# x comes transposed as well, the first column group multiplies it before the norm, and u is normalised in place

## The chip, the cores and the metric

The kernel runs on one core of a Trainium2 chip. The metric is the device time of one execution in microseconds, as the median of several runs. Four engines are named below: TensorE (PE in the profile; PEld is its weight loads), VectorE (DVE), ScalarE (ACT) and GpSimd (POOL). SyncE (SP) issues the transfers, one after the other.

## The reference

One layer takes 512 tokens and 16 meta tokens of width 1024 in fp32, normalises them, projects them to eleven column groups, runs a retention branch and a gated linear attention (GLA) branch on them, merges the two, adds the residual and normalises again. What bears on the change is its start:

```python
u = rms_norm(h, norm_gain)          # u = h * r * gain, r = 1/sqrt(mean(h*h) + eps) per token
proj = u @ w_in
(rq, rk, rv, rg, gq, gk, gv, gg, glr, m_ret, m_gla) = jnp.split(proj, points, axis=-1)
...
gq = gq.reshape(bsz, length, GLA_HEADS, GLA_K_DIM) * (GLA_K_DIM ** -0.5)
gk = gk.reshape(bsz, length, GLA_HEADS, GLA_K_DIM)
gv = gv.reshape(bsz, length, GLA_HEADS, GLA_V_DIM)
log_a = jax.nn.log_sigmoid((glr @ w_gate_up + b_gate)) / GLA_GATE_TAU
```

Since r is one number per token, (h * gain) @ w scaled row by row with r is the same product as u @ w.

## The kernel before

**Products.** Every fp32 product is made from three products of reduced precision. `split` (L139 to 141) casts a tile to a high part on ACT (L140) and subtracts it from the tile on another engine, DVE unless told otherwise, for the low part (L141). `mm3` (L152, L155, L156) multiplies high by high, low by high and high by low. Six buffers hold raw weights, three hold high and low parts. PSUM has two pools of four banks, `pp` and `pa`.

**Tokens.** The 528 tokens are held as two halves of 264 (256 tokens and 8 meta tokens). The activations lie transposed, as 128 features by 264 tokens, four such blocks side by side. `fh` and `fl` hold their high and low parts in seven forms: A11, A12, A22 and (as `a21h`, `a21l`) A21 are the blocks of u, S1 to S4 are sums and differences of them, which `quad` uses to make a 2 by 2 block product with seven products instead of eight.

**The start, in program order.** x is loaded in four blocks of 128 rows and one of 16 meta rows (L409 to 419), each followed on SP by a piece of the first weight, `gv0`. Then for every block (L435 to 455): squares and their sum on ACT (L436), r by `rstd_of` on DVE and POOL (L163, L164), the multiply `xn` = x * r * gain on DVE with the gain broadcast to all partitions (L439), eight transposes of 128x128 on TensorE (L444), and from their PSUM banks the split into fh and fl and a copy into `u` (L452, L453). Then the four sums (L472 to 475) and their splits.

**After that.** `forget_gates` loads its small weight (`fg_f`, L492), multiplies u by it (`glr`, 32 products), then makes the gate logits `z` (five products) and from them `la` through exponentials and logarithms on ACT and DVE. `gla_v(0)` makes the first 512 columns of gv with `proj_b` (96 products of 128x512, in four pieces `gv_0` to `gv_3` of the weight) and the meta rows (`gv_pm`, 8 products). `gla_qk(0)` makes gq and gk with `proj_a` (96 products each). Then `gla_g(0)`, a `quad` (products gg_1, gg_2, gg_6, gg_7, gg_5 and so on, 24 each), runs together with `gla_attention(0)`: `ge`, `gf` (sums of la, from its high and low parts `lah`, `lal`), `gm` (the same for the meta rows), `gc` (scores from gQ and gK). The other column groups, the retention branch, the merge and the output projection follow.

**What sets the order.** `weave` takes turns between a generator of products and one of a chain of small steps: one step of the chain for each step of the products, from the third argument on. Within that, the tile framework places instructions on each engine's queue; an engine works its queue in order. `pin` holds the products of one group behind those of the one before. A tile taken from a pool whose memory another tile still uses waits for that tile's last reader: the pool `gp` lies over the memory of `xp`, which holds x, xn, the sums and the other tiles of the start.

Of the kernel before, what the change touches and what calls it, by code (L numbers as in the profile page):

```python
# [106 lines left out]
def hybrid_kernel(ctx: ExitStack, tc: tile.TileContext, I, out: bass.AP):  # L107
# [23 lines left out]
    ggain = cp.tile([P, 16], F32, name="ggain")  # L131
# [43 lines left out]
    def run(*gens):  # L175
        for g in gens:
            yield from g
# [139 lines left out]
    def proj_b(src, col, left, name, evac, meta=None):  # L317

        pss = [ppt(f"{name}_p{t}") for t in range(NTB)]
        psm = pat(f"{name}_pm") if meta is not None else None  # L320
        raws = []
        for q in range(4):
# [4 lines left out]
            if name == "gv0":  # L327
                for kk in range(2):
                    split(hi[:, kk, :], lo[:, kk, :], raw[:, kk, :], nc.gpsimd)
            else:  # L330
                split(hi, lo, raw)
            raws.append(raw)
            for t in range(NTB):
                for kk in range(2):
                    k = 2 * q + kk
                    mm3(pss[t], *left(k, t), hi[:, kk, :], lo[:, kk, :], k == 0, k == KD - 1, True)
                if q == 3:
                    evac(t, pss[t])
                if t == 1:
                    run_late()  # L340
                    yield
            if psm is not None and q % 2 == 1:
                for g in range(4):
                    k = 2 * (q - 1) + g
                    nc.tensor.matmul(psm[32 * g:32 * g + 32], um[:, k, :], raws[q - 1 + g // 2][:, g % 2, :],
                                     start=q == 1, stop=q == 3)
            if q == 3 and psm is not None:
                late.append(lambda: meta(psm))
            yield

# [52 lines left out]
    gmask = g1.tile([P, 3, P], I32, name="gmask")  # L403

# [4 lines left out]
    blocks = [(I["x"][t * P:(t + 1) * P, :], P, t * P) for t in range(NTB)]  # L409
    blocks.append((I["meta_tokens"], NM, T))  # L410
    xts = []
    ngb = xp.tile([P, D], F32, name="ngb", bufs=1)
    for n, (src, rows, t0) in enumerate(blocks):
        xts.append(xp.tile([P, D], F32, tag="xt", name=f"xt{n}", bufs=5))
        nc.sync.dma_start(xts[n][:rows], src)
        if n == 0:
            nc.sync.dma_start(ngb, I["norm_gain"].to_broadcast([P, D]))
        if n < NTB:
            load_b(w_in, C_GV, n, "gv0")
# [3 lines left out]
    wps = pat("warm_p")  # L423

    def warm(n):
        for _ in range(n):
            nc.tensor.matmul(wps, wzero[:, :P], wzero, start=True, stop=True)

    warm(14)
    nc.gpsimd.memset(um, 0.0)  # L430
    u = xp.tile([P, 2, 2, 4, HT], F32, name="u", bufs=1)
    for n, (src, rows, t0) in enumerate(blocks):
        xt = xts[n]
        sq = xp.tile([P, D], F32, tag="sq", name=f"sq{n}")
        ss = sp.tile([P, 1], F32, tag="ss", name=f"ss{n}")  # L435
        nc.scalar.activation(sq[:rows], xt[:rows], AF.Square, accum_out=ss[:rows])  # L436
        r = rstd_of(ss[:rows], D, rows, f"n{n}")
        xn = xp.tile([P, D], F32, tag="xn", name=f"xn{n}")
        nc.vector.scalar_tensor_tensor(xn[:rows], xt[:rows], r[:rows], ngb[:rows], op0=ALU.mult, op1=ALU.mult)  # L439
        for g in range(2):  # L440
            pt = pat(f"xt{n}_{g}")
            for e in range(4):
                k = 4 * g + e
                nc.tensor.transpose(pt[:, e * P:e * P + rows], xn[:rows, k * P:(k + 1) * P], ident[:rows, :rows])  # L444
            v = pt.rearrange("p (e t) -> p e t", e=4)[:, :, :rows]
            if rows == NM:
# [7 lines left out]
        if n == 0:  # L454
            warm(3)
# [621 lines left out]
```

## Time and profile before

| what | us |
|---|---|
| median of 3 runs | 822.55 (821.91 to 823.01) |
| the profiled execution, its own time | 823.74 |
| its span in the trace | 822.0 |
| TensorE busy in the span | 790.3 |
| first gv0 product | 10.89 |
| gate logits z | 55.10 |
| first gg product | 86.02 |
| second gg_b group (gg_5) | 102.52 |

The span is what the trace covers; the execution's own time is 1.7 longer. A row of a timeline gives start, duration, engine, source line, operation, output tile<-operand tiles, shape and count, and in brackets the idle time of the engine ahead of it with what ended it. A wait of several things is put down to the last of them.

### The profile page before, as it was taken

What the parts mean: (1) busy time and instruction counts of PE and PEld (TensorE: products, weight loads), DVE (VectorE), ACT (ScalarE), POOL (GpSimd) and SP (SyncE); (2) the same over time, 40 slices, a digit from 0 to 9 for tenths busy, and PEclk for the clock granted to TensorE, in tenths of its full rate; (3) what the DMA queues carried; (4) which work ended last, traced back from release to release, by engine and by line L of the source; (5) the groups of instructions that cost most, each with busy time, mean ns of one, the idle gap of its engine ahead of it and who ended that gap; (6) DMA issues with size and microseconds to landing.
All of it is one profiled execution on the core that took longest, in us unless ns stands there. A gap on an engine that the chain in (4) does not pass through costs nothing.

```text
span 822.0 us, 13635 instructions
## 1 busy us (share of the span) xinstructions
PE 790.3 (96%) x5466; PEld 719.3 (88%) x5466; DVE 541.5 (66%) x775; ACT 407.7 (50%) x673; POOL 147.3 (18%) x186
## 2 busy tenths in 40 slices
PE   6898999999999999999999999999999998999896
PEld 3687988998887999998999989999899998998685
DVE  3758666577643398766677576766757778885922
ACT  6564585357744336525445354453444555553422
POOL 4500243005331240013000141002410010021031
PEclk9998999999999999999999999999999999999999
DMA  9240330033335803521426237261472267589402
GB/s 282 82 115 26 90 90 3 26 103 103 111 120 143 193 26 103 176 82 65 143 76 185 72 72 151 66 198 57 85 146 71 84 218 230 179 184 249 146 0 103
DMA packets 84679, 95.62 MB, mean 116 GB/s; under 512 B 7988, under 2 KB 71732, under 8 KB 84616
## 3 DMA queue, kind: packets, MB, share of 16 engines
q1 hardware_dynamic: 78984, 86.36, 34.4%
q0 software_dynamic: 5632, 8.39, 7.0%
q8 instruction: 43, 0.70, 0.4%
q14 instruction: 20, 0.16, 0.1%
HBM read 77.96 MB, written 16.78 MB: 115 GB/s over the span
## 4 chain that ended last, share of the span: by engine, by line
PE 75%; DVE 6%; DMA 4%; ACT 4%; issue 2%; POOL 2%; SPq 0%; POOLq 0%; DVEq 0%; ACTq 0%
PE rk_p L297 6%; PE rg_b L225 6%; PE rq_p L297 6%; PE rv_b L225 5%; PE gk_p L297 3%; PE rg_c L225 3%; PE br_p L155 3%; PE br_p L152 3%; PE br_p L156 3%; PE rv_c L225 2%; PE mg_b L225 2%; DMA mk<-kept 2%; PE gg_b L225 2%; PE wo_p L152 2%; PE wo_p L156 2%
## 5 line engine op out<-in xcount | busy, mean ns | idle before, releaser
L164 POOL TENSOR_TENSOR g_r<-g_v,mhalf 128x1 f32<-128x1 f32 x16 | 10.3, 646 | 265.4 <-DVE g_v L163 265.4
L152 PE MATMUL br_p<-oh,br_h 128*128 128x512 f32 x128 | 50.1, 391 | 0.5 <-DVE mt L974 0.5
L155 PE MATMUL br_p<-ol,br_h 128*128 128x512 f32 x128 | 50.3, 393 | 0.0
L156 PE MATMUL br_p<-oh,br_l 128*128 128x512 f32 x128 | 50.1, 391 | 0.0
L141 DVE TENSOR_TENSOR rg_l<-rg_w,rg_h 128x1024 fp32r<-128x1024 f32 x24 | 30.0, 1252 | 17.9 <-ACT rg_h L140 17.9
L141 DVE TENSOR_TENSOR rv_l<-rv_w,rv_h 128x1024 fp32r<-128x1024 f32 x24 | 29.4, 1224 | 15.8 <-ACT rv_h L140 15.8
L914 ACT ACTIVATE on<-av,nm,g_r 128x512 f32<-128x512 f32 x16 | 12.5, 778 | 52.6 <-DVE nm L912 52.6
L140 ACT CAST rv_h<-rv_w 128x1024 fp32r<-128x1024 f32 x24 | 25.3, 1052 | 23.9 <-issue 7.3
L225 PE MATMUL rv_b<-rv_h,fh 128*128 128x256 f32 x128 | 36.3, 284 | 0.0
L225 PE MATMUL rg_b<-rg_l,fh 128*128 128x256 f32 x128 | 36.0, 281 | 0.0
L225 PE MATMUL rv_b<-rv_h,fl 128*128 128x256 f32 x128 | 36.0, 281 | 0.0
L225 PE MATMUL rv_b<-rv_l,fh 128*128 128x256 f32 x128 | 36.0, 281 | 0.0
L140 ACT CAST rg_h<-rg_w 128x1024 fp32r<-128x1024 f32 x24 | 25.2, 1052 | 21.6 <-PE br_p L155 11.6
L225 PE MATMUL rg_b<-rg_h,fl 128*128 128x256 f32 x128 | 35.9, 281 | 0.0
L225 PE MATMUL rg_b<-rg_h,fh 128*128 128x256 f32 x128 | 35.8, 280 | 0.0
L639 POOL COPY gto<-gX 128x1 f32<-128x1 f32 x16 | 8.5, 530 | 122.9 <-ACT gX L629 122.9
L152 PEld LDWEIGHTS br_p<-oh,br_h 128*128 128x128 f32 x128 | 24.0, 188 | 6.1 <-issue 0.9
L638 POOL TENSOR_TENSOR gQ<-gX,gq 128x512 f32<-128x512 f32 x16 | 28.3, 1768 | 3.9 <-ACT gX L631 3.9
L152 PE MATMUL wo_p<-wo_h,mh 128*128 128x512 f32 (+1 forms) x72 | 26.9, 374 | 2.0 <-DVE mt L974 2.0
L156 PEld LDWEIGHTS br_p<-oh,br_l 128*128 128x128 f32 x128 | 24.0, 188 | 5.2
L155 PEld LDWEIGHTS br_p<-ol,br_h 128*128 128x128 f32 x128 | 24.0, 188 | 5.0
L297 PE MATMUL rk_p<-fh,rk_h 128*128 128x264 f32 x96 | 27.6, 287 | 0.0
(490 smaller groups left out, 3098.2 us busy)
## 6 DMA issues: line engine op xcount, KB each, us to landing
rg_w<-in_w_in_dram SPq DMA_DIRECT2D x16, 512.0 KB, 4.2
rv_w<-in_w_in_dram SPq DMA_DIRECT2D x16, 512.0 KB, 3.9
br_w<-in_w_branch_ret_dram SPq DMA_DIRECT2D x16, 512.0 KB, 4.1
gv_w<-in_w_in_dram SPq DMA_DIRECT2D x8, 512.0 KB, 3.6
gg_w<-in_w_in_dram SPq DMA_DIRECT2D x8, 512.0 KB, 4.5
bg_w<-in_w_branch_gla_dram SPq DMA_DIRECT2D x8, 512.0 KB, 3.5
rq_w<-in_w_in_dram SPq DMA_DIRECT2D x8, 512.0 KB, 4.2
rk_w<-in_w_in_dram SPq DMA_DIRECT2D x8, 512.0 KB, 4.6
```

Of the source, the lines that this page charges most:

```text
L140: nc.scalar.copy(hi, src)
L141: eng.tensor_sub(lo, src, hi.bitcast(F32))
L152: m = nc.tensor.matmul(o, lh, rh, start=first, stop=False)
L155: nc.tensor.matmul(o, lh, rl, start=False, stop=False)
L156: m = nc.tensor.matmul(o, ll, rh, start=False, stop=last)
L164: nc.gpsimd.tensor_tensor(r[:rows], v[:rows], mhalf[:rows], op=ALU.pow)
L225: m = nc.tensor.matmul(ps[:, t, :], l, r, start=first and j == 0, stop=kk == 3 and j == 2, skip_group_check=not fresh or t == 1)
L297: m = nc.tensor.matmul(pss[t][th], l[:, kk, c], r, start=first and j == 0, stop=kh == 1 and kk == 3 and j == 2, skip_group_check=not meta ...
L638: nc.gpsimd.tensor_mul(Q[b, h], X[:, 0:4, :], qb)
L639: nc.gpsimd.tensor_copy(TO[b, h], X[:, 0, P - 1:P])
L914: nc.scalar.activation(on, ps, AF.Identity, scale=r, bias=nm)
```

## The change

The host hands over x a second time, transposed and in the two halves with their meta tokens (`xt`, 128 x 8 x 2 x 264), and the three gains laid out by column. The transposed x goes straight into `u`. From it come `xgh` and `xgl`, the high and low parts of x * gain, made by eight instructions on ACT and eight on DVE. gv0 multiplies these, without the norm, and its evacuation on ACT scales each token's row by r.

The norm runs beside that in a new generator, `activations`. x in rows is still loaded for its squares. r stands on the diagonal of a tile `dg`; a matrix of ones times `dg` leaves r in all partitions of a PSUM bank `rb`; 16 instructions on DVE multiply u by gain and `rb` in place. fh and fl of u are then split from u in blocks of 128x1056, and the sums are made in the buffer of `xgh`. The 32 transposes, the copies into u, the broadcast load of the gain (512 KB) and the tiles `xn` go. The low parts of gv0's weights are subtracted on DVE instead of POOL. The meta rows of gv0 follow its last product in one run of eight. The first twelve products on zeros, which run before data is there, replace 14 + 3. `gla_v(0)` is woven with `activations`, and `forget_gates` with `gla_qk(0)` alone. `gv` and `gvm` move to a pool of their own memory, since `gp` is opened later.

```diff
     def proj_b(src, col, left, name, evac, meta=None):
...
             if name == "gv0":
                 for kk in range(2):
-                    split(hi[:, kk, :], lo[:, kk, :], raw[:, kk, :], nc.gpsimd)
+                    split(hi[:, kk, :], lo[:, kk, :], raw[:, kk, :])
...
-            for t in range(NTB):
-                for kk in range(2):
-                    k = 2 * q + kk
-                    mm3(pss[t], *left(k, t), hi[:, kk, :], lo[:, kk, :], k == 0, k == KD - 1, True)
-                if q == 3:
+            steps = [(t, kk) for t in range(NTB) for kk in range(2)]
+            if q == 0:
+                steps.sort(key=lambda x: x[1])
+            for n, (t, kk) in enumerate(steps):
+                k = 2 * q + kk
+                mm3(pss[t], *left(k, t), hi[:, kk, :], lo[:, kk, :], k == 0, k == KD - 1, True)
+                if q == 3 and kk == 1:
                     evac(t, pss[t])
...
+        if meta is not None:
+            psm = pat(f"{name}_pm")
+            for k in range(KD):
+                g = k % 4
+                nc.tensor.matmul(psm[32 * g:32 * g + 32], um[:, k, :], raws[k // 2][:, k % 2, :],
+                                 start=k < 4, stop=k >= 4)
...
+    nc.sync.dma_start(ng, I["norm_gain"])
+    for q in range(4):
+        nc.sync.dma_start(u[:, 2 * q:2 * q + 2], I["xt"][:, 2 * q:2 * q + 2])
+        load_b(w_in, C_GV, q, "gv0")
+        for n in ((), (0, 1), (2, 3), ())[q]:
+            nc.sync.dma_start(xr[n], I["x"][n * P:(n + 1) * P, :])
+        if q == 1:
+            nc.sync.dma_start(xr[4][:NM], I["meta_tokens"])
...
+    for k in range(KD):
+        g = ng[:, k:k + 1]
+        nc.scalar.activation(xgh[:, k], u[:, k], AF.Copy, scale=g)
+        nc.vector.scalar_tensor_tensor(xgl[:, k], u[:, k], g, xgh[:, k].bitcast(F32),
+                                       op0=ALU.mult, op1=ALU.subtract)
...
+    def norm(n, rows=P):
         ss = sp.tile([P, 1], F32, tag="ss", name=f"ss{n}")
+        nc.scalar.activation(xr[n][:rows], xr[n][:rows], AF.Square, accum_out=ss[:rows])
+        norms[n] = rstd_of(ss[:rows], D, rows, f"n{n}")
+        dg = xp.tile([P, P], F32, tag="dg", name=f"dg{n}", bufs=3)
+        nc.vector.tensor_scalar_mul(dg[:rows, :rows], ident[:rows, :rows], norms[n][:rows])
+        return dg
+
+    def activations():
+        dgm = norm(4, NM)
+        for th in range(2):
+            rb = pat(f"rb{th}")
+            for i in range(2):
+                nc.tensor.matmul(rb[:, i * P:(i + 1) * P], ones, norm(2 * th + i), start=i == 0, stop=True,
+                                 skip_group_check=i > 0)
...
+            for g in range(2):
+                for k in range(4 * g, 4 * g + 4):
+                    nc.vector.scalar_tensor_tensor(u[:, k, th, :], u[:, k, th, :], ng[:, k:k + 1], rb[:, :HT],
+                                                   op0=ALU.mult, op1=ALU.mult)
+                split(ah[th, g][:, :, :HT], al[th, g][:, :, :HT], u[:, 4 * g:4 * g + 4, th, :])
+            nc.vector.tensor_copy(um[:, :, th * HM:(th + 1) * HM], u[:, :, th, 256:HT])
+            yield
...
+        sums = xp.tile([P, KD, 2, HT], F32, tag="xgh", name="sums", bufs=1).rearrange("p (i k) h t -> p i (k h) t", i=4)
...
+            split(fh[i][:, :, :HT], fl[i][:, :, :HT], ss[i])
+            yield
...
         if p == 0:
-            yield from proj_b(w_in, C_GV, left, "gv0", lambda t, ps: nc.scalar.copy(v[:, t, :], ps), meta)
+            yield from proj_b(w_in, C_GV, left, "gv0", lambda t, ps: nc.scalar.activation(
+                v[:, t, :], ps, AF.Copy, scale=norms[t]), meta)
...
+    weave(gla_v(0), activations(), 3)
+    xctx.close()
+    gp = gctx.enter_context(tc.tile_pool(name="gp", bufs=1, reuse_waits="tile"))
...
-    weave(run(gla_v(0), gla_qk(0)), forget_gates(), 4)
+    weave(gla_qk(0), forget_gates(), 1)
```

Three places show how instructions move. The first is the split of gv0's last weight piece, `gv_3_l`. Before, it stood on POOL; its neighbours there are small casts of constants and the meta rows' norm (`n_r`):

```order
L141 TENSOR_TENSOR gv_2_l<-gv_2_w,gv_2_h 128x512 x2
L465 CAST sel<-sel_raw 128x128
L466 CAST gsum<-gs_raw 128x640
L467 CAST gsm<-gsm_raw 16x16
L164 TENSOR_TENSOR n_r<-n_v,mhalf 16x1
L141 TENSOR_TENSOR gv_3_l<-gv_3_w,gv_3_h 128x512 x2
```

Now it stands on DVE in two halves, with the norm of the second half of the tokens between them (`rb_317` is the second broadcast of r, `fl_88` and `a21l` are low parts of u):

```order
L142 TENSOR_TENSOR gv_3_l<-gv_3_w,gv_3_h 128x512
L448 TENSOR_SCALAR dg_324<-ident,n_r 128x128
L448 TENSOR_SCALAR dg_333<-ident,n_r 128x128
L142 TENSOR_TENSOR fl_88<-u,fh_81 128x4x264
L463 SCALAR_TENSOR_TENSOR u<-u,ng,rb_317 128x264 x7
L142 TENSOR_TENSOR a21l<-u,a21h 128x4x264
L463 SCALAR_TENSOR_TENSOR u<-u,ng,rb_317 128x264
L142 TENSOR_TENSOR gv_3_l<-gv_3_w,gv_3_h 128x512
```

The second half of the split has moved behind eight multiplies and two splits of u; TensorE's last gv0 products read it.

The second place is DVE between the sums and the low parts of gq's weight (`gq_0_l`, `gq_1_l`) and of the gates' weight (`fg_w`). Before:

```order
L473 TENSOR_TENSOR s_300<-u 128x1056
L141 TENSOR_TENSOR fl_92<-s_302,fh_85 128x4x264
L474 TENSOR_TENSOR s_301<-s_300,u 128x1056
L141 TENSOR_TENSOR fl_90<-s_300,fh_83 128x4x264
L475 TENSOR_TENSOR s_303<-u,s_301 128x1056
L141 TENSOR_TENSOR fl_91<-s_301,fh_84 128x4x264
L141 TENSOR_TENSOR gq_0_l<-gq_w_575,gq_0_h 128x1024
L141 TENSOR_TENSOR fl_93<-s_303,fh_86 128x4x264
L502 TENSOR_TENSOR fg_w<-fg_f,fg_w 128x8x16
```

Now, on the same engine, with `gvm_l` for the meta rows of gv0:

```order
L142 TENSOR_TENSOR gq_0_l<-gq_w_434,gq_0_h 128x1024
L142 TENSOR_TENSOR fl_89<-u,fh_82 128x4x264
L475 TENSOR_TENSOR sums<-u 128x1056 x2
L142 TENSOR_TENSOR fl_92<-sums,fh_85 128x4x264
L475 TENSOR_TENSOR sums<-sums,u 128x1056
L142 TENSOR_TENSOR fl_90<-sums,fh_83 128x4x264
L475 TENSOR_TENSOR sums<-u,sums 128x1056
L142 TENSOR_TENSOR fl_91<-sums,fh_84 128x4x264
L142 TENSOR_TENSOR gvm_l<-gv_pm,gvm_h 128x512
L142 TENSOR_TENSOR fl_93<-sums,fh_86 128x4x264
L142 TENSOR_TENSOR gq_1_l<-gq_w_540,gq_1_h 128x1024
```

`gq_1_l` now stands ahead of the gates' split and behind all four sums; the sums wait for the last reader of `xgh`.

The third place is TensorE at the first scores of the attention (`gc`), beside the product gg_6 of the gate columns. Before, the scores followed the last gg_6 product (lines 648 to 650):

```order
L225 MATMUL gg_b<-gg_6_h,fh_84 128x256
L225 MATMUL gg_b<-gg_6_l,fh_84 128x256
L225 MATMUL gg_b<-gg_6_h,fl_91 128x256
L648 MATMUL gc_988<-gQ_886,gK_887 128x128
L649 MATMUL gc_988<-gQ_886,gK_887 128x128
L650 MATMUL gc_988<-gQ_886,gK_887 128x128
```

Now they follow the first of them (lines 660 to 662):

```order
L679 MATMUL gm_910<-gsm,lal_901 128x16
L226 MATMUL gg_b<-gg_6_h,fh_84 128x256
L660 MATMUL gc_947<-gQ_845,gK_846 128x128
L661 MATMUL gc_947<-gQ_845,gK_846 128x128
L662 MATMUL gc_947<-gQ_845,gK_846 128x128
L660 MATMUL gc_957<-gQ_861,gK_862 128x128
L661 MATMUL gc_957<-gQ_861,gK_862 128x128
L226 MATMUL gg_b<-gg_6_l,fh_84 128x256
```

Five of the six score products have moved ahead of 23 of gg_6's 24 products.

More of the change, by code (lines that the diff above doesn't have):

```diff
@@ L423, in hybrid_kernel @@
     wps = pat("warm_p")
[L425 to L429, printed above, removed]
+    for _ in range(12):
+        nc.tensor.matmul(wps, wzero[:, :P], wzero, start=True, stop=True)
+    ones = xp.tile([P, P], F32, name="ones", bufs=1)
+    nc.gpsimd.memset(ones, 1.0)
     nc.gpsimd.memset(um, 0.0)
[L431 to L434, printed above, removed]
[L435 to L455 removed]
@@ L568, in gla_v @@
     def gla_v(p):
[L569 removed]
+        v = gv[p]
         G["v", p] = v
```

74 lines of the change are left out of this document (29 added, 45 removed).

## The prediction

> **What bounds the kernel now.** I read the page's first parts, then the chain of work that ended last, then the timeline of each engine up to 105 us, then windows for the granted clock. First the page:
>
> ```profile
> span 822.0 us, 13635 instructions
> PE 790.3 (96%) x5466; PEld 719.3 (88%) x5466; DVE 541.5 (66%) x775; ACT 407.7 (50%) x673; POOL 147.3 (18%) x186
> PE   6898999999999999999999999999999998999896
> PEclk9998999999999999999999999999999999999999
> PE 75%; DVE 6%; DMA 4%; ACT 4%; issue 2%; POOL 2%; SPq 0%; POOLq 0%; DVEq 0%; ACTq 0%
> ```
>
> TensorE is busy 96% of the span and carries 75% of the chain. Only the first slices (20.6 us each) and the last show it less busy, and the change touches the first five. From the second group of gg products on, TensorE's order is the same in both kernels, so I take the start of that group as a **checkpoint**: what arrives earlier there ends earlier. The way to it, on TensorE (start us, duration us, engine, line, operation, tile<-operands, count, idle before and its releaser):
>
> ```profile
> 10.89 0.50 PE L152 MATMUL gv_p<-gv_h,fh 128*128 128x512 f32 x1 [1.91 <-ACT fh L140]
> ...
> 26.44 0.64 PE L444 MATMUL xt<-ident,xn 16*128 16x16 f32 x8 [1.28 <-DVE xn L439]
> ...
> 36.47 0.50 PE L152 MATMUL gv_p<-gv_h,fh 128*128 128x512 f32 x1
> ...
> 46.31 0.39 PE L152 MATMUL gv_p<-gv_h,fh 128*128 128x512 f32 x1
> ...
> 51.34 0.28 PE L511 MATMUL glr<-fl,fg_w 128*128 128x264 f32 x1
> ...
> 52.71 1.06 PE L345 MATMUL gv_pm<-gv_w,um 128*32 128x512 f32 x8
> ...
> 55.10 1.08 PE L521 MATMUL z<-fg_r 128*128 128x512 f32 x4
> ...
> 69.75 0.39 PE L624 MATMUL ge<-gsum,lah 128*128 128x256 f32 x1 [2.36 <-ACT lah L140]
> ...
> 86.02 0.28 PE L225 MATMUL gg_b<-gg_h,fh 128*128 128x256 f32 x1
> ...
> 89.27 0.34 PE L628 MATMUL gf<-gsum,lal 128*128 128x384 f32 x1
> ...
> 95.84 0.39 PE L648 MATMUL gc<-gQ,gK 128*128 128x128 f32 x2
> ...
> 99.17 0.33 PE L657 MATMUL gc<-ident,gK 128*128 128x128 f32 x1 [0.78 <-DVE stb L654]
> ...
> 102.52 0.28 PE L225 MATMUL gg_b<-gg_h,fh 128*128 128x256 f32 x1
> ```
>
> The first gv product waits until 10.89 for the chain load, square, norm, transpose, split of the first 128 rows of x. From 36.47 to 46.31 lie 42 products, 0.234 us each. The gate rows `z` follow at 55.10; the checkpoint is 102.52. The rest of the start hangs on DVE, ACT and the loads:
>
> ```profile
> 12.86 1.28 DVE L141 TENSOR_TENSOR fl<-xt,fh 128x512 fp32r<-128x512 f32 x2
> ...
> 34.90 1.25 DVE L141 TENSOR_TENSOR fl<-s,fh 128x1056 fp32r<-128x1056 f32 x1
> 36.06 1.24 DVE L474 TENSOR_TENSOR s<-s,u 128x1056 f32<-128x1056 f32 x1
> ...
> 50.27 0.48 DVE L516 SCALAR_TENSOR_TENSOR fg_r<-glr,fg_f,fg_r 32x256 fp32r<-32x256 f32 x1 [2.93 <-ACT fg_r L515]
> ...
> 82.44 0.42 DVE L599 COPY gk<-gk_p 128x264 f32<-128x264 f32 x1
> 82.79 1.21 DVE L261 TENSOR_TENSOR gg_w<-gg_w,gg_t 128x1024 f32<-128x1024 f32 x1
> ```
>
> ```profile
> 4.32 1.06 ACT L436 ACTIVATE sq<-xt 128x1024 f32<-128x1024 f32 x1 [2.32 <-DMA xt<-in_x_dram]
> ...
> 46.71 0.70 ACT L501 CAST fg_w<-fg_f 128x128 fp32r<-128x128 f32 x3 [1.01 <-DMA fg_f<-in_w_in_dram]
> ...
> 60.50 1.03 ACT L140 CAST gk_h<-gk_w 128x1024 fp32r<-128x1024 f32 x1
> ...
> 69.30 0.40 ACT L140 CAST lah<-la 128x256 fp32r<-128x256 f32 x1
> ```
>
> ```profile
> 7.92 0.34 SPq L461 DMA_DIRECT2D sel_raw<-in_sel_dram  x1
> ...
> 14.49 0.38 SPq L469 DMA_DIRECT2D rgain<-in_ret_norm_gain_dram  x1
> ...
> 42.45 0.50 SPq L492 DMA_DIRECT2D fg_f<-in_w_in_dram  x1
> ```
>
> A 128x1056 DVE subtraction is followed 1.16 us later by the next (34.90 to 36.06); two of 128x512 take 1.28, so one about 0.6. SP, each issue held behind a landing, takes five steps between 7.92 and 14.49: 1.31 us for a piece of 0.5 MB.
>
> **The change part by part.** All times are of the profiled execution: 823.74, that is 822.0 of span and 1.7 around it, 1.2 above the median 822.55.
>
> *Start of gv0.* Norm, transposes and u copies leave the way of the first product. It needs the first piece of transposed x (the first 0.5 MB landed at 4.32; now a small load goes ahead and the piece is a little larger: 5.0), the weight piece 1.31 later (6.3) and one cast of about 0.6: 7.0 instead of 10.89. The 48 products of the first two weight pieces end at 7.0 + 48 x 0.234 = 18.2, with 0.3 of gaps 18.5. The `rb0` broadcast of r adds 0.4. The 24 of the third piece end at 24.5. The 32 transposes of 128x128 and the late meta transposes (26.44), with their half clock, are gone.
>
> *The new queue on DVE.* The split of the fourth piece's second half, `gv_3_l`, stands on DVE behind the norm of both halves of u. A multiply of 128x264 with a PSUM operand is not shown. The 264 copy from PSUM gives the stage free after 0.35 (82.44 to 82.79), the 32x256 multiply-type instruction at 50.27 took 0.48. I take 0.36, by the row of the same shape; 16 times the 0.12 to the other end are 1.9 us. Below 0.35 no row of this width goes. From `rb0` at 19.1: 8 multiplies of the first half 2.9, two xgl 1.25, fl splits 1.16 twice, two n_v, um, dg 1.1, first half of gv_3_l 0.6, then 8 multiplies of the second half 2.9, a21l 1.16, second half of gv_3_l 0.6: 12.8, that is 31.9. TensorE meanwhile ends the third piece and `rb1` and stands at 27.0 until 32.0: a **new wait of 5 us**. Twenty products are left.
>
> ```profile
> 27.00:28.00 1.00, 1.00 (x4) 0.83 (x3) 0.76 (x3) 0.99 (x2) 0.00 (x0) 0.50 0.00 0
> ...
> 72.00:74.00 2.00, 2.00 (x9) 2.00 (x10) 2.00 (x2) 0.00 (x0) 0.00 (x0) 0.50 0.00 0
> 74.00:76.00 2.00, 2.00 (x11) 2.00 (x10) 1.97 (x4) 0.40 (x1) 0.00 (x0) 0.50 0.84 255
> 76.00:78.00 2.00, 2.00 (x11) 2.00 (x10) 2.00 (x2) 0.00 (x0) 0.00 (x0) 0.50 0.05 15
> 78.00:80.00 2.00, 2.00 (x18) 2.00 (x17) 0.00 (x1) 0.00 (x0) 0.00 (x0) 0.97 0.00 0
> ```
>
> These windows give start and end, width, busy time and count of PE, PEld, DVE, ACT and POOL, then granted clock, DMA share, GB/s. After the wait at 69.75 the clock is 0.50 from 72 to 78, about 10 products in 2 us instead of 18. Two pieces of the chain of waits price that stretch:
>
> ```profile
> 71.92 14.26 PE gk_p L297 x92
> 86.18 2.85 PE gg_b L225 x24
> ```
>
> 24 products took 2.85, so 0.119 each at full clock; 92 of the same kind took 14.26 where 0.12 each make 11.0: 3.2 lost. After my 5 us wait I take 2.2 of that (between nothing and 3.2, nearer to the row; only 20 products are left there), so the last gv product ends at 38.8 instead of 36.6. The Trainium skill, "TensorE: Matmul & The Clock Gate", section "What's actually happening", has the clock halved after an idle window of about 3.4 us and restored after a busy one, in windows that run free of the kernel. By that rule alone only the 5 us wait would cost about one such window, and the sum would be some 2 us lower; but the 0.50 at 27 us follows a gap of only 1.28 (26.44), and the rows decide.
>
> *Sums and gq.* gv_pm, all eight now together, costs its 1.06: 39.9. The first half of gq is 48 products at 0.12 (the 32 glr products up to 51.34 took 3.9): 45.7. The sums lie in xgh's buffer, so DVE starts them only behind the last gv product: 38.7, then four sums and four fl splits at 1.16 to 1.25 and gvm_l 0.6 give 48.8, and gq_1_l behind them 49.9. TensorE waits about 4 us. The gates' load also waits for the last of these splits, since its tile lies over xp: 48.8 + 4.2 (42.45 to 46.71) = 53.0, and 1.0 of casts: 54.0. The 27 gq products between hide under it, even at half clock. glr 54.1 to 58.0, and z 3.6 behind it as before (51.5 to 55.1): **61.6, 6.5 later than 55.10**. But then 75 of the 96 gq products lie ahead of the gates (the other 21, 2.5 us, fill the 3.6), and DVE has the gq and gk splits behind it.
>
> *From z to the checkpoint.* Before, lah came 14.2 after z (55.10 to 69.30), TensorE idle 2.36 ahead of the first ge. Two gk_h casts (60.50, 1.03 each) there now lie earlier, and the chain beside them on DVE hides a little of that: 12.6. gk's 96 products at 0.12 and a small rest take 11.8 and hide under it. The first gg product needs a PSUM slot that gk's copies on DVE free, and these stand behind la's subtractions: z + 15.5 = 77.1 (86.02 before). From there to the checkpoint before took 16.5, with one wait of 0.78 (99.17): the scores `gc` stand behind four stretches of other work, the last of them the 24 products of gg_6. Now they stand behind the first gg_6 product. Their operands came 6.6 us after the last gf product (89.27 to 95.84), and TensorE will be there after two groups less: 24 gg_2 products of 0.119 each, gm and one gg_6, 3.7 us. So 2.9 of new wait, and about 0.5 of the old 0.78 goes, as more products follow: 18.9, and 0.5 of half clock. 77.1 + 18.9 + 0.5 = **96.5**.
>
> The gain is 102.5 - 96.5 = 6.0 us: 823.7 - 6.0 = 817.7 for the profiled kind of execution, and 822.55 - 6.0 = 816.5 on the median. POOL is rid of the gv_l splits, DVE takes them (8 x 0.6, counted above where they stand in the way). The final stages are untouched.
>
> **Rivals.**
>
> 1. *The clock stays full and the waits come out shorter.* No half clock behind the new waits (2.2 and 0.5) and 0.8 of the queues hidden: gain 9.5, 813.0. For it: the later slices of the page stay at 9 although TensorE shows 8 in several. Against it: 0.50 from 72 to 78 after one wait of 2.36. Chance 0.20.
> 2. *More half clock.* The first wait and the one at the first gg product each lose the 3.2 which the wait at 69.75 lost: 1.0 and 2.7 over my sum, gain 2.3, 820.2; with the wait at gq_1_l the same (3.2 more) 823.4. For it: the windows. Against it: behind gq_1_l TensorE waits for the gates' load anyway. Chance 0.15, of which 0.09 stays below 820.9.
> 3. *Slower: the queue ahead of gv_3_l runs as slowly as DVE did beside POOL.* One instruction of before, of the shape that otherwise takes 1.24, took 2.35 while POOL made a split:
>
> ```profile
> 32.62 2.35 DVE L473 TENSOR_TENSOR s<-u 128x1056 f32<-128x1056 f32 x1
> ```
>
> ```profile
> 30.29 3.56 POOL L141 TENSOR_TENSOR gv_l<-gv_w,gv_h 128x512 fp32r<-128x512 f32 x2 [5.30 <-ACT gv_h L140]
> ```
>
> At 1.9 times its durations the queue of 12.8 takes 24.3, the wait grows by 11.5, and 816.5 becomes 828.0. It decides from 1.47 times (6.0 us); for the multiplies alone that would be 0.74 each. Against it: the four splits on POOL are what the change takes away, and POOL holds little else there. Chance 0.07.
> 4. *The start is hidden anyway:* the chain from z to the checkpoint (lah, exponentials) sets the time and z comes 6.5 later, so that nothing is left: 822.5. For it: lah, not a product, ended the wait at 69.75. Against it: 10 us of TensorE's work now lie ahead of z instead of behind it, and from 71.92 on TensorE's pieces of the chain follow each other without a wait. Chance 0.03.
>
> **How the numbers follow.** Forecast 0.55, rivals 0.20, 0.15, 0.07, 0.03. About 0.2% (1.65 us) is what a measurement of this kernel can tell from no change. Faster holds the forecast, rival 1 and 0.09 of rival 2: 0.84. Same (820.9 to 824.2) holds the rest of rival 2 and rival 4: 0.09. Slower, rival 3: 0.07. The range goes from 811.5 (rival 1 with another 1.5 off the new 5 us wait) to 821.0 (the multiplies at their upper end, 1.9, and 2.7 of clock at the first gg product).
>
> **What would show it.** Right: first gv product near 7.0, rb0 near 18.5, a TensorE wait of about 5 us ended by DVE gv_3_l at 32, last gv product near 38.8, a wait of about 4 us ended by gq_1_l near 50, glr at 54, z near 61.6, first gg near 77, the next gg_b group near 96.5, and from there on the same distances as before. Wrong: multiplies over 0.48 us, a first product after 8.5, z after 65, a clock of 0.50 in more than three stretches before 100 us, or a gain at the checkpoint that is given back behind it.

## The result, and the profile after

| | before | changed |
|---|---|---|
| median of 4 runs, us | 822.23 (821.41 to 823.01) | 832.64 (831.58 to 835.06) |
| ratio of the runs | 1 | 1.0131, 95% interval 1.0105 to 1.0157 |
| span of the profiled execution, us | 822.0 | 829.8 |

The changed kernel is slower by 10.4 us, where 6.0 us less were forecast. Four executions of the runs below took far longer than the rest (1092.72 and 1963.08 us in e8, the second of them the profiled one; 1283.66 in e3; 2714.24 in the kernel before) and stand in the medians, while the ratios leave them out. The page of the profile after, first its span, its engines and the chain that ended last:

```profile
span 829.8 us, 13572 instructions
PE 791.9 (95%) x5433; PEld 720.0 (87%) x5433; DVE 549.5 (66%) x799; ACT 408.3 (49%) x661; POOL 135.0 (16%) x179
PEclk9899899999999999999999999999999999999999
PE 74%; DVE 8%; issue 6%; DMA 6%; ACT 2%; POOL 2%; SPq 1%; POOLq 0%; DVEq 0%; ACTq 0%
```

DVE's share of the chain rose from 6% to 8%, and the second and the fifth slice (20 to 41 and 83 to 104 us) show the clock at 8. The places of the prediction on TensorE, in the timeline after:

```profile
8.51 0.50 PE L153 MATMUL gv_p<-gv_h,xgh 128*128 128x512 f32 x1 [2.03 <-ACT gv_h L141]
...
22.07 0.61 PE L457 MATMUL rb<-dg,ones 128*128 128x128 f32 x4
...
37.29 0.80 PE L156 MATMUL gv_p<-gv_l,xgh 128*128 128x512 f32 x1 [4.52 <-DVE gv_l L142]
...
55.11 0.58 PE L298 MATMUL gq_p<-fh,gq_l 128*128 128x256 f32 x1 [1.79 <-DVE gq_l L142]
...
66.47 0.70 PE L533 MATMUL z<-fg_r 128*128 128x512 f32 x2
...
82.29 0.58 PE L226 MATMUL gg_b<-gg_h,fh 128*128 128x256 f32 x1 [2.13 <-DVE gk L611]
...
94.49 0.49 PE L660 MATMUL gc<-gQ,gK 128*128 128x128 f32 x2 [1.86 <-POOL gQ L650]
...
105.21 0.28 PE L226 MATMUL gg_b<-gg_h,fh 128*128 128x256 f32 x1
```

The first product comes 2.4 us earlier than before, the checkpoint 2.7 us later. Following every TensorE product from one trace to the other (offset of the same product, after less before):

| place | time before, us | offset, us |
|---|---|---|
| checkpoint, second gg_b group | 102.5 | +2.7 |
| gq of the second pair of heads | 140.8 | +3.1 |
| GLA's output projection bg, start of its long run | 235.2 | +3.1 |
| its last product | 274.6 | +3.9 |
| output products of the retention branch | 758.3 | +4.0 |
| output projection wo0, first product | 767.3 | +4.4 |
| wo0, second half | 788.6 | +7.6 |

So the loss lies mainly in two places: at the start, where a gain was forecast, and in wo0, which the prediction took as untouched. Up to the checkpoint TensorE waits 17.7 us (14.2 before) and loses 8.7 us to half clock while it works (6.5 before); its work at full clock is 3.0 us less. That adds up to the 2.7. The four wo0 products that had to wait for a bank, before and after:

```profile
767.29 0.39 PE L152 MATMUL wo_p<-wo_h,mh 128*128 128x512 f32 x1
...
769.60 0.50 PE L152 MATMUL wo_p<-wo_h,mh 128*128 128x512 f32 x1 [0.38 <-DVE mt L974]
...
772.53 0.50 PE L152 MATMUL wo_p<-wo_h,mh 128*128 128x512 f32 x1 [1.27 <-DVE mt L974]
...
774.51 0.50 PE L152 MATMUL wo_p<-wo_h,mh 128*128 128x512 f32 x1 [0.32 <-DVE mt L974]
```

```profile
771.70 0.42 PE L153 MATMUL wo_p<-wo_h,mh 128*128 128x512 f32 x1
...
773.52 0.50 PE L153 MATMUL wo_p<-wo_h,mh 128*128 128x512 f32 x1 [0.93 <-DVE mt L989]
...
776.46 0.50 PE L153 MATMUL wo_p<-wo_h,mh 128*128 128x512 f32 x1 [1.98 <-DVE mt L989]
...
778.43 0.71 PE L153 MATMUL wo_p<-wo_h,mh 128*128 128x512 f32 x1 [1.01 <-DVE mt L989]
```

The fourth bank comes 3.9 later, about the offset that the stage arrived with (4.4). What differs is what fills the time between the banks. `proj_b` makes wo0 too, and the line `if q == 0: steps.sort(...)` has no condition on the name: before, each bank was followed by six products (both 128-feature steps), now by three, and after the fourth bank 15 products are left instead of six. At 0.23 us each nine products are 2.1 us, and the clock falls behind the longer waits, which loses 1.7 (windows of after; columns as in the prediction):

```profile
777.00:780.00 3.00, 1.99 (x6) 1.28 (x5) 2.97 (x6) 1.64 (x3) 0.00 (x0) 0.76 0.00 1
780.00:783.00 3.00, 3.00 (x11) 2.33 (x10) 2.58 (x3) 0.00 (x0) 0.00 (x0) 0.67 0.00 0
```

### The profile page after: what moved, and what is told of

Same layout as the page of the kernel before. It is cut to its first block, busy times and chain, and to the rows that moved or that the text cites. A ratio compares the mean times of both kernels' runs of the same rounds, so it can differ in the third digit from the quotient of the medians.

```text
span 829.8 us, 13572 instructions
## 1 busy us (share of the span) xinstructions
PE 791.9 (95%) x5433; PEld 720.0 (87%) x5433; DVE 549.5 (66%) x799; ACT 408.3 (49%) x661; POOL 135.0 (16%) x179
## 4 chain that ended last, share of the span: by engine, by line
PE 74%; DVE 8%; issue 6%; DMA 6%; ACT 2%; POOL 2%; SPq 1%; POOLq 0%; DVEq 0%; ACTq 0%
PE rk_p L298 6%; PE rv_b L226 6%; PE rg_b L226 5%; PE rq_p L298 5%; PE rv_c L226 3%; PE rg_c L226 3%; PE br_p L156 3%; PE br_p L157 3%; PE br_p L153 3%; PE gg_b L226 2%; PE gq_p L298 2%; PE wo_p L153 2%; PE wo_p L156 2%; PE wo_p L157 2%; PE bg_p L156 2%
## 5 line engine op out<-in xcount | busy, mean ns | idle before, releaser
L153 PE MATMUL br_p<-oh,br_h 128*128 128x512 f32 x128 | 49.9, 390 | 0.9 <-DVE mt L989 0.9
L929 ACT ACTIVATE on<-av,nm,g_r 128x512 f32<-128x512 f32 x16 | 12.4, 778 | 52.6 <-DVE nm L927 52.6
L298 PE MATMUL rk_p<-fh,rk_l 128*128 128x264 f32 x96 | 27.4, 285 | 0.0
```

The source lines that it names most:

```text
L153: m = nc.tensor.matmul(o, lh, rh, start=first, stop=False)
L298: m = nc.tensor.matmul(pss[t][th], l[:, kk, c], r, start=first and j == 0, stop=kh == 1 and kk == 3 and j == 2, skip_group_check=not meta ...
L929: nc.scalar.activation(on, ps, AF.Identity, scale=r, bias=nm)
```

## The experiments

Thirteen kernels ran. All times are medians with the ratio to the kernel before on the same chip, whose median was between 822.7 and 822.8 us each time. Single executions of one kernel otherwise differ by 2 to 6 us, so one profile shows where a stretch moved and the ratio what it is worth.

| run | edit | median, us | ratio (95% interval) |
|---|---|---|---|
| e1 | changed, sort in gv0 only | 828.6 | 1.0076 (1.0058 to 1.0094) |
| e2 | before, sort in wo0 | 827.1 | 1.0056 (1.0036 to 1.0075) |
| e3 | e1, table load ahead | 827.57 | 1.0057 (1.0036 to 1.0078) |
| e4 | e1, sums apart | 825.4 | 1.0045 (1.0025 to 1.0064) |
| e5 | e1, gv_3 split early | 827.01 | 1.0046 (1.0029 to 1.0062) |
| e6 | e1, gv_3 split on GpSimd | 826.73 | 1.0046 (1.0031 to 1.0061) |
| e7 | e3, e4 and e5 together | 826.33 | 1.0044 (1.0029 to 1.0059) |
| e8 | e5 without 14 multiplies of u | 820.76 | 0.9975 (0.9962 to 0.9988) |
| e9 | e1, gg wait filled | 826.69 | 1.0052 (1.0034 to 1.0071) |
| e10 | before, ge wait filled | 822.7 | 0.9995 (0.9981 to 1.0009) |
| e11 | before, gv moved in memory | 822.22 | 0.9994 (0.9981 to 1.0006) |
| e12 | e3, row-wise x first | 828.46 | 1.0076 (1.0063 to 1.0089) |
| e13 | e12 with sums apart | 825.7 | 1.0036 (1.0022 to 1.0049) |

### The order in wo0: e1 and e2

```diff
-            if q == 0:
+            if q == 0 and name == "gv0":
                 steps.sort(key=lambda x: x[1])
```

> The changed kernel, but the new order of a first weight piece's products (all four token groups for its first 128 features, then all four for its second) only in gv0 and no longer in wo0, the output projection, which goes through the same function. Theory A: that order costs 3.7 us in wo0 (the offset of TensorE against before grows from 4.0 to 7.7 there), because a fourth PSUM bank comes free late and 15 products instead of 6 are left behind it: 832.6 - 3.7 = 828.9, and TensorE's offset stays at 4.0 to the end. Rival: the loss at the end comes from elsewhere (the placing of tiles, the landing of kept rows): 832.6.

> The kernel before, with that one order of products in wo0 and nothing else. Theory A: 822.2 + 3.7 = 825.9. Rival (the loss needs the rest of the change): 822.2.

e2 puts the same sorted steps into the kernel before, for wo0 alone. The ratio falls from 1.0131 to 1.0076 in e1 and rises from 1 to 1.0056 in e2: 4.5 and 4.6 us of 822, one effect from both sides (the intervals of the changed kernel and e1 don't overlap, nor those of e2 and before). In e2's trace the three later banks come with the same waits (1.08, 1.97 and 0.54), and TensorE's offset to before goes from +0.1 at 767 us to +4.4 at 783. Theory A is shown; its price was put 0.8 too low. What is left of the loss in e1 is 0.76% (0.58 to 0.94), some 6 us.

### The first product: e3

```diff
     nc.vector.memset(wzero, 0.0)
+    nc.scalar.activation(sp.tile([P, 1], F32, tag="rv", name="early"), mhalf, AF.Copy, scale=mhalf)
```

> e1 with one tiny activation on ACT ahead of everything, so that the table which the scaled copy needs is loaded before the transposed x lands and not behind it (1.28 us at 5.29). Theory B: the first gv0 product comes at 7.2 instead of 8.5, TensorE's gap ahead of it falls from 2.0 to 0.7, the half clock from 10 to 14 us goes (2 us), rb0 comes at 18.8 instead of 22.1, and all of it reaches the end: 828.9 - 3.3 = 825.6. Rival: the half clock stays, since shorter gaps bring it too: 827.6. Second rival: the DVE queue ahead of gv_3_l is bound by the landing of the last piece of x, and nothing reaches the end: 828.9.

ACT loads a table ahead of its first activation. In the kernel before that was done at 2.0 us; in the changed one it stood behind the landing of the first piece of x. The timeline of ACT, before and after:

```profile
0.72 1.28 ACT L436 ACT_TABLE_LOAD   x1 [0.72 <-PEq L1067]
```

```profile
5.29 1.28 ACT L438 ACT_TABLE_LOAD   x1 [5.29 <-DMA u<-in_xt_dram]
6.58 1.36 ACT L438 ACTIVATE xgh<-u,ng 128x528 fp32r<-128x528 f32 x2
```

The next two rows show TensorE in e3, and the windows below it the clock of the same stretch, after first and e3 second:

```profile
6.97 0.50 PE L153 MATMUL gv_p<-gv_h,xgh 128*128 128x512 f32 x1 [0.50 <-ACT gv_h L141]
...
18.95 0.38 PE L458 MATMUL rb<-dg,ones 128*128 128x128 f32 x2
...
23.29 0.68 PE L156 MATMUL gv_p<-gv_l,xgh 128*128 128x512 f32 x1 [2.28 <-DVE gv_l L142]
...
35.69 0.79 PE L156 MATMUL gv_p<-gv_l,xgh 128*128 128x512 f32 x1 [4.05 <-DVE gv_l L142]
```

```profile
10.00:12.00 2.00, 2.00 (x7) 1.59 (x6) 2.00 (x5) 1.27 (x3) 0.00 (x0) 0.64 1.04 349
12.00:14.00 2.00, 2.00 (x6) 1.52 (x6) 0.63 (x2) 1.25 (x3) 0.00 (x0) 0.51 1.00 374
```

```profile
10.00:12.00 2.00, 2.00 (x11) 1.59 (x10) 1.08 (x2) 0.15 (x1) 0.00 (x0) 1.00 1.05 330
12.00:14.00 2.00, 2.00 (x10) 1.65 (x9) 0.14 (x1) 1.67 (x3) 0.19 (x1) 1.00 1.01 392
```

The Trainium skill, "ScalarE: Activation LUTs", section "What ACT_TABLE_LOAD costs", gives 1283 ns for the load, and the traces agree; that a load can wait behind the first operand is what the sum missed.

The first half of theory B held: first product at 6.97, no half clock from 10 to 14, rb0 3.1 us earlier. The second half fell. gv_2_l now stood late on DVE (a wait of 2.28 at 23 us, and half clock from 23.4 to 26.9 behind it), gv_3_l came only 1.6 earlier, the checkpoint 1.8 earlier (102.57 against 104.36 in e1), and by the two ratios the time fell by 1.6, with intervals that overlap.

### The sums and gv_3_l: e4 to e7

e4 puts the sums into the buffers of the row-wise x; e5 asks for the split of gv_3 beside that of gv_2; e6 gives gv_3_l to GpSimd; e7 is e3, e4 and e5.

```diff
-        sums = xp.tile([P, KD, 2, HT], F32, tag="xgh", name="sums", bufs=1).rearrange("p (i k) h t -> p i (k h) t", i=4)
...
-            ss[i] = sums[:, len(ss)]
+            ss[i] = xp.tile([P, 4 * HT], F32, tag="xr", name=f"s{i}", bufs=4).rearrange("p (k t) -> p k t", k=4)
```

```diff
+                if q == 2:
+                    w3 = loaded[name, 3]
+                    for kk in range(2):
+                        split(ahead[0][:, kk, :], ahead[1][:, kk, :], w3[:, kk, :])
```

```diff
-                    split(hi[:, kk, :], lo[:, kk, :], raw[:, kk, :])
+                    split(hi[:, kk, :], lo[:, kk, :], raw[:, kk, :], nc.gpsimd if q == 3 else nc.vector)
```

> e1 with the four sums in the memory of the row-wise x (done with by 20 us) instead of that of xgh. Theory C: the sums no longer wait for the last gv0 product (4.2 us of idle DVE ahead of them), so gq_1_l, the gates' load, glr and z come 4 us earlier, TensorE's wait for gq_1_l (1.8) and the half clock behind it go, and the first gg product comes 4 us earlier: 828.9 - 4.0 = 824.9. Rival: the sums get in front of gv_3_l on DVE, the wait of 4.5 us there grows by what is saved, and nothing is won: 828.9 or more.

> e1 with the split of gv0's last weight piece asked for together with that of the third piece, so that both halves of gv_3_l stand on DVE ahead of the norm of the second half of u. Theory D: the wait of 4.5 us for gv_3_l at 37 us and the half clock behind it (36 to 41 us) go, the last gv0 product comes near 36 instead of 44; but DVE's own queue (the u multiplies, the splits, the sums up to gq_1_l, all in one line with only 4.2 us idle in it, ahead of the sums) sets z, so only those 4.2 us reach the end: 828.6 - 4.2 = 824.4, and TensorE stands in front of gq_1_l for longer instead. Rival: TensorE's own waits set the time, and 4.5 of wait and 2 of half clock reach the end: 822.1. Second rival: the place where gv_3_l stands doesn't matter: 828.6.

> e1 with gv_3_l on GpSimd, as in the kernel before. Theory D: the same as e5 and 1.3 us less on DVE, 823.1, unless the multiplies of u beside it slow down. Rival: DVE beside GpSimd takes 1.9 times as long for the 3.5 us of the split, which gives 1.7 back: 824.8.

> e3, e4 and e5 together. Theory D (DVE's queue from rb0 to gq_1_l sets z): rb0 3 us earlier as in e3 and no idle stretch ahead of the sums, so z comes 7 us earlier than in e1: 828.6 - 3.1 - 4.2 = 821.3, level with the kernel before. Rival (each gain covers the same wait): 825.4, as e4 alone. Second rival: the stretch from z to the second gg_b group, with its waits for gk's copies and for gQ and its half clock, takes up what comes earlier: over 824.

TensorE's places in those traces, in us:

| run | first gv product | last gv product ends | z | first gg | checkpoint | waits up to the checkpoint |
|---|---|---|---|---|---|---|
| before | 10.9 | 52.8 | 55.1 | 86.0 | 102.5 | 14.2 |
| e1 | 8.4 | 43.5 | 64.6 | 80.4 | 104.4 | 17.7 |
| e4 | 8.3 | 47.1 | 64.6 | 81.2 | 102.7 | 17.2 |
| e5 | 8.2 | 36.6 | 64.0 | 79.9 | 103.8 | 16.7 |
| e6 | 8.3 | 39.1 | 65.4 | 81.3 | 104.1 | 16.1 |
| e7 | 7.4 | 38.2 | 64.5 | 80.3 | 103.1 | 17.0 |
| e13 | 7.0 | 45.7 | 63.3 | 79.9 | 103.6 | 19.6 |

Among the changed kernels here the end of gv0 moves by up to 10 us, z by about two, the checkpoint by less than two. In e5 the wait of 4.52 at 37 us is gone as expected, and a wait of 5.12 for gq_1_l stands at 50.9 in its place. Two rows of e7's timeline show the same exchange:

```profile
51.48 0.58 PE L298 MATMUL gq_p<-fh,gq_l 128*128 128x256 f32 x1 [4.41 <-DVE gq_l L142]
...
80.32 0.58 PE L226 MATMUL gg_b<-gg_h,fh 128*128 128x256 f32 x1 [2.68 <-DVE gk L618]
```

All four come out at 1.0044 to 1.0046, so that e4 to e7 are not told apart and each is at most 2.6 us under e1, with intervals that overlap. The expectation for e7 that the gains add up (821.3) is false; its first rival, that they cover the same wait (825.4), came nearest, and the second (over 824) fits the time as well. e5 and e6 miss theory D's 824.4 and 823.1 by 2.6 and 3.6. In e6 one split of u beside GpSimd's work took 1.94 instead of 1.25, and DVE then stood idle for GpSimd's n_r (1.85) and for ACT's a21h (3.14). e4's time is near theory C's 824.9, but z did not come 4 us earlier, as that theory has it: the sums did get in front of gv_3_l, as e4's rival says, and the last gv product ended at 47.1 instead of 43.5.

### What holds gq_1_l: e8, e12 and e13

The chain of waits of the changed kernel names DVE from rb0 on (start, us, what):

```profile
23.43 2.08 DVE u L463 x5
25.51 1.36 DVE xgl L439 x2
27.27 1.17 DVE fl L142
28.99 1.61 POOL n_r L165 x2
30.62 0.64 DVE dg L448
32.15 2.89 DVE u L463 x7
35.04 1.20 DVE a21l L142
36.63 0.61 DVE gv_l L142
37.29 0.80 PE gv_p L156
43.82 2.43 DVE sums L475 x2
...
53.84 1.23 DVE gq_l L142
55.11 4.18 PE gq_p L298 x21
59.29 3.87 PE glr L523 x32
```

e8 takes work out of that queue:

```diff
-                for k in range(4 * g, 4 * g + 4):
-                    nc.vector.scalar_tensor_tensor(u[:, k, th, :], u[:, k, th, :], ng[:, k:k + 1], rb[:, :HT],
-                                                   op0=ALU.mult, op1=ALU.mult)
+                if g == 0:
+                    nc.vector.scalar_tensor_tensor(u[:, 0, th, :], u[:, 0, th, :], ng[:, 0:1], rb[:, :HT],
+                                                   op0=ALU.mult, op1=ALU.mult)
```

> e5 with 14 of the 16 multiplies of u by gain and r left out, so that most of u stays un-normalised. Theory D (DVE's queue from rb0 to gq_1_l sets z): 14 x 0.40 = 5.6 us less on DVE, TensorE's wait of 5 us for gq_1_l goes, z comes 5 us earlier and so does the second gg_b group: 827.0 - 5.0 = 822.0. Rival: the gates' load, not DVE's queue, holds glr and z (it waits for the last split of the sums and then needs 4 us), so half of it is lost: 824.5. Second rival: the stretch from z to the second gg_b group takes it up: 827.

820.76 us, by the ratio 0.25% (0.12 to 0.38) under the kernel before, and by the two ratios 5.8 us less than e5, give or take 1.7. The 5.6 us of DVE work reach the end about whole, as theory D says, and neither rival fits. So the work on DVE in this stretch is paid for in the time: that is shown. That it is paid through gq_1_l and z is argued, since no trace of e8 shows on which wait the 5.8 us are gained. e8 leaves most of u un-normalised; only its times are used.

e12 and e13 leave the work and start it earlier: the row-wise x is loaded beside the first two weight pieces, and the norm asked for after a piece and a half.

```diff
-        for n in ((), (0, 1), (2, 3), ())[q]:
+        for n in ((0, 1), (2, 3), (), ())[q]:
...
-    weave(gla_v(0), activations(), 3)
+    weave(gla_v(0), activations(), 2)
```

> e3 with the row-wise x (for the squares) loaded beside the first two weight pieces instead of the second and third, and the norm of u asked for after a piece and a half of gv0 instead of two. Theory G (z is set by when u is done: the last split of u ends at 39.6 us in the changed kernel and 30.8 in the one before, and what follows on DVE up to gq_1_l is about as long in both): rb0 comes near 15 instead of 19 to 22, DVE's idle time between 12 and 23 us is used, u is done near 34; the sums still wait for gv0's last product, so about 2 us reach the end: 825.6. Rival: the later pieces of x and of the weight land 5 us later, TensorE waits for them in gv0, and nothing is won: 827.6 or more.

> e12 and e4 together: the sums no longer wait for gv0 either. Theory G: DVE's queue runs from 15 us to gq_1_l with no idle stretch ahead of the sums, z comes 6 to 7 us earlier than in e3 and the second gg_b group 5: 827.6 - 5.0 = 822.6, level with the kernel before (with the earlier table and the order in wo0 in it). Rival: TensorE is short of data in gv0 and of work behind z, 825.4 as in e4.

rb0 came at 13.6 in e12, and the last split of u ended at 34.7 instead of 39.6. But the splits of gv0's weights now stood behind the multiplies, TensorE waited 8.05 us for one at 32.9, gv0 ended at 45.6, and the sums behind it started at 45.4 (43.8 in the changed kernel). 828.46 us: e12's rival has the time right, though the wait was for a split on DVE and not for a landing. e13 frees the sums from that wait; gq_1_l ended at 50.5 instead of 55.1, z came at 63.3, and yet the checkpoint at 103.6 and the median at 825.7, the value of its rival. An earlier start alone isn't worth what e8's smaller queue is: theory G falls, at least in this form.

DVE's queue is not all that sets z, either. gq_1_l ends at 54.6 in e1 and at 51.7, 50.8, 51.4 and 50.5 in e4, e5, e7 and e13: 2.9 to 4.1 earlier. z comes at most 1.3 earlier. In e5 and e7 the gates' load, issued behind the last split of the sums, starts at 52.0 and 52.6, only 1.4 and 0.8 earlier than in e1 (53.5). In e4 and e13 it starts at 49.7 and 47.4, but TensorE's order has changed with the edit: 24 gq products stand between the two halves of glr and 24 more ahead of z, where e1 has the 32 glr products in a row and then 23 of gq and four of gk.

### The clock behind a wait: e9 and e10

```diff
                 nc.tensor.matmul(pf[:, :384], lah[:, hc:hc + P], gsum[:, 256:], start=True, stop=False)
+                if p == 0 and b == 0 and h == 1:
+                    for _ in range(24):
+                        nc.tensor.matmul(pf[:, 384:], wzero[:, :P], wzero[:, :P], start=True, stop=True, skip_group_check=True)
```

e10 has 30 of them ahead of the first ge product of the kernel before. In e9 they fall between the two halves of one head's sums in the same bank and change the decays of that head's first block: by the Trainium skill, "PSUM — Partial Sum Buffer", section "The four PSUM rules", a product that starts an accumulation clears the state of its whole bank, which fits, and no run here isolates it.

> e1 with 24 small products on zeros in TensorE's queue between the first ge/gf products and the first gg product, where it waits 2.1 us for gk's copies and then runs at half clock from 82 to 86 us. They write an unused part of a PSUM bank. Theory E (the idle stretch brings the half clock): the clock stays at 1.00 there and 2.0 us go: 826.6. Rival: the clock falls all the same, or what is gained waits at the gQ wait behind: 828.6.

> The kernel before with 30 such products ahead of its first ge product, where TensorE waits 2.36 us for lah and then runs at half clock from 72 to 78 us. Theory E: the clock stays at 1.00 there and 3 us go: 819.7. Rival: the clock falls all the same: 822.7.

Windows of after (its later stretches of half clock up to the checkpoint), then of e9, then of e10 (its stretch from 72 us on, which the prediction shows at 0.50 for the kernel before):

```profile
38.00:40.00 2.00, 2.00 (x6) 1.54 (x5) 1.64 (x2) 0.69 (x1) 0.00 (x0) 0.50 0.15 25
...
56.00:58.00 2.00, 2.00 (x11) 2.00 (x11) 1.53 (x3) 0.70 (x3) 0.03 (x1) 0.50 0.29 57
...
82.00:84.00 2.00, 1.71 (x8) 1.71 (x9) 2.00 (x6) 0.30 (x1) 0.00 (x0) 0.56 0.00 0
84.00:86.00 2.00, 2.00 (x12) 2.00 (x12) 1.86 (x2) 0.11 (x1) 0.00 (x0) 0.59 0.00 0
...
96.00:98.00 2.00, 2.00 (x12) 2.00 (x11) 1.23 (x2) 0.77 (x1) 0.00 (x0) 0.50 0.00 0
```

```profile
82.00:84.00 2.00, 2.00 (x18) 2.00 (x19) 2.00 (x5) 0.41 (x1) 0.00 (x0) 1.00 0.00 0
84.00:86.00 2.00, 2.00 (x18) 2.00 (x18) 1.78 (x4) 1.00 (x2) 0.00 (x0) 1.00 0.00 0
```

```profile
72.00:74.00 2.00, 2.00 (x19) 2.00 (x18) 2.00 (x4) 0.29 (x1) 0.00 (x0) 1.00 0.26 52
74.00:76.00 2.00, 2.00 (x19) 2.00 (x18) 1.97 (x3) 0.12 (x1) 0.00 (x0) 1.00 0.60 210
```

Filled waits kept the clock at 1.00 in both profiles. Three profiles with the order of before and no filling (before, e2, e11) all have half clock behind this wait, and of nine changed kernels without filling, eight have it behind the gg wait. So the idle stretch brings the half clock here; this rests on one profile of each filled kernel, and it is no fixed rule: in e4 the gg wait was longer (2.60) and unfilled, and the clock stayed at 1.00. By the Trainium skill, "TensorE: Matmul & The Clock Gate", section "What's actually happening", an idle window halves the clock, and these traces agree as to idleness; but the windows before and after show it behind waits of about 2 us, shorter than the 3.4 us that the page gives for a window. The times don't follow the profiles: e10's median is that of the kernel before (single runs from 819.3 to 824.0, the profiled one 819.75), and e9's is 1.9 under e1 with intervals that overlap. Whether filling a wait is worth anything over many executions stays open; e10 says at most 0.2%.

### The place of gv in memory: e11

In every changed kernel but e8, where it was not measured, the products of bg follow each other in 0.2326 to 0.2335 us (the longest unbroken run of 91, by the timeline), in the four with the old start (before, e2, e10, e11) in 0.2275 to 0.2278. That is 0.9 us over the stage, at a granted clock of 1.00 in both. e11 moves gv and gvm in the kernel before as the change does (with one buffer of the squares fewer, and one constant beside them, to make room):

```diff
-        v = gp.tile([P, NTB, 512], F32, tag="gv", name=f"gv{p}")
+        v = gv[p]
```

> The kernel before with gv and gvm in the pool of their own memory as in the changed kernel, which moves every later tile of the GLA branch in memory; the order of instructions is that of before on TensorE, DVE and ACT. Theory F: the place in memory makes the products of GLA's output projection (bg) slower: 0.2315 us from one to the next instead of 0.2265, as in every changed kernel, 0.85 us in all: 823.5. Rival: their rate comes from something else that the change brought: 0.2265 and 822.7.

0.2277: theory F falls for gv and gvm. Whether the place of another tile matters is not tested; what makes these products slower is open.

## Why the prediction was wrong, point by point

1. **First product, 7.0 forecast, 8.51 measured.** The sum had the landing and the cast right but no table load (1.28 us, ACT at 5.29). e3 without it: 6.97.
2. **rb0, 18.5 forecast, 22.07 measured.** 1.5 of it is point 1. Most of the rest is half clock from 10.6 to 14.0 us behind the longer gap, 1.7, which the sum did not hold; e3 removes both and gives 18.95. Its mechanism (a gap, then half clock) was one that the prediction used further on.
3. **The queue ahead of gv_3_l, 12.8 us forecast.** Measured from the first multiply at 23.02 to 37.24: 14.2. A multiply was put at 0.36 and took 0.40 to 0.41 (7 in 2.89), within its bounds; the other 0.7 is DVE idle for GpSimd's n_r. The wait of 5 us was 4.52. Right in mechanism, and near in size.
4. **gq_1_l, glr, z.** Forecast 49.9, 54.1 and 61.6, measured 55.1, 59.1 and 66.5: each 5 late, as much as points 1 to 3 bring (1.5, 2.1 and 1.4). Two things inside went otherwise. The wait ahead of gq_1_l was put at 4 and measured 1.79, since TensorE came later too (the eight meta products took 1.93 and not 1.06); DVE ends it, so nothing moved. And glr came 4.1 behind gq_1_l, where 4.2 were forecast, but not for the gates' load: that took 2.3 instead of 4.2, the gates' weight was ready at 57.5, and the gq products at half clock held TensorE until 59.1. That the two agree is luck. The first gg product at z + 15.5 came at z + 15.8.
5. **From the first gg product to the checkpoint, 19.4 forecast, 22.9 measured.** The waits were sized right (3.2 in all; 0.71, 1.86, 0.64 and 0.26 measured). The half clock was not: 0.5 was taken, and a mean granted clock of 0.85 over these 22.9 us is 3.4. This is rival 2's mechanism; it priced this place at 2.7 over the sum, and 2.9 came.
6. **What no step held.** The sorted steps reach wo0 through `proj_b`: 4.5 us, shown by e1 and e2. A row's name in the order, `wo_p<-wo_h,mh`, does not tell which 128 features it multiplies, and the diff's `q == 0` does. The bg products added 0.9.

Points 1, 2, 3 and 5 turn a gain of 6.0 at the checkpoint into a loss of 2.7: 5.2 up to the first gg product (82.29 against 77.1) and 3.5 behind it. One profile is not a mean: the kernel before passed the checkpoint at 102.5 in its profile, at 101.3 in e2 and at 99.9 in e11, which have its order up to there, so the loss at the start is 2.7 to 5.3 us. With wo0's 4.5 and bg's 0.9 that is 8.1 to 10.7, and 10.4 was measured. Of the prediction's signs of being wrong three came: a first product after 8.5, z after 65, and half clock in five stretches before 100 us, where it allowed three.

So two steps failed. The first is the premise *"From the second group of gg products on, TensorE's order is the same in both kernels"*, and with it *"The final stages are untouched"*: in wo0 the order differs, and that costs 4.5 us. The second is the sum up to the checkpoint, above all its term for the half clock: 2.7 us (2.2 behind gv_3_l and 0.5 behind the scores) against 8.7 measured, in five stretches (10.6 to 14.0, 34.4 to 41.3, 54.9 to 58.3, 82.2 to 85.6 and 95.9 to 99.3 us). Its 2.2 was near: 2.0. Of the other four stretches the sum held the one behind gq_1_l to be hidden, and the rest came to 0.5.

Behind the second stands where the normalised u is made. gv0's products start earlier, but all other products need u, and that is done later: the last split of u ends on DVE at 39.6 us, and ended at 30.8 before (two rows of DVE, after and before):

```profile
38.39 1.25 DVE L142 TENSOR_TENSOR fl<-u,fh 128x1056 fp32r<-128x1056 f32 x1
```

```profile
30.60 0.19 DVE L141 TENSOR_TENSOR fl<-xt,fh 128x32 fp32r<-128x32 f32 x1
```

From there a queue on DVE leads to gq_1_l and to the gates' load. e8 shows that its length counts; e5 and e7 show that where one wait of TensorE is freed and the queue stays, the wait moves to the next product. How much of the start's loss is this queue, how much the half clock behind its waits and how much TensorE's order ahead of z, the runs do not separate. Of the rivals, the third (DVE slowed as beside GpSimd) had the right sign and the wrong mechanism: no multiply took longer than 0.48 us, the queue took 14.2 and not 24.3, and it was late by its start.

No version of the changed kernel with its output whole beats the kernel before; e13 comes nearest, 0.36% behind it, and e4 to e7 follow at 0.44 to 0.46%.

## What to carry to other kernels

When the first product of a kernel is made independent of a slow preparation, ask when the second group of products gets its operands: if the preparation then runs later or on a fuller engine, the gain ends with the first group. Where a wait goes and the engine behind it stays as full, look for the same wait at the next product before counting the gain. Read a changed helper for every caller: a condition that was meant for the first stage cost 4.5 us in the last.

## What the runs showed of the hardware that was not expected

The bg products run 2% slower in every changed kernel that was measured (0.2326 to 0.2335 us against 0.2275 to 0.2278) at the same granted clock, with an order that is the same; memory placement of gv is not the cause (e11), and none was found.

Half clock appeared behind a wait of 2.03 us at the start (0.51 from 12 to 14 us) and not behind one of 0.50 (e3). No length of a wait decides it in these runs: 1.66 us brought it at the start of e7 (from 8.2 to 11.7 us), 1.75 did not at the start of e13, and 2.60 did not ahead of the first gg product in e4. Up to the checkpoint each stretch of half clock lasted 3.41 us or two or three times that, in every trace but e8's, so that each such 3.41 us loses up to 1.7.
